# One product-key query over 512 tokens in place of two over 256, and gate steps twice as close

## The chip, the cores and the metric

The kernel runs on one core of one Trainium2 chip. The metric is device time in microseconds (us) of one execution. The kernel before takes 3155.48 us, the median of 3 runs (3149.81 to 3155.99).

The profile names the engines PE (matrix products; PEld its weight loads), DVE (VectorE), ACT (ScalarE), POOL (GpSimd) and SP (SyncE, which issues most transfers). Each works through its own instructions in order. L217 is line 217 of the kernel.

## The reference

One layer for a sequence of 1024 tokens with 1024 channels, in float32. The first half mixes tokens: a convolution group and a recurrent group (RWKV-7) read one input projection, and their outputs go through an output projection and a layer norm. The second half is a retrieval over 128 x 128 = 16384 one-neuron experts (PEER). Cut to what matters here:

```python
h2 = adaln(x, shift2, scale2)
q = (h2 @ peer_wq).reshape(bsz, seq, PEER_HEADS, PEER_QDIM).astype(jnp.float32)
...
s1 = jnp.einsum('bshd,hnd->bshn', q[..., :half], peer_k1.astype(jnp.float32))
s2 = jnp.einsum('bshd,hnd->bshn', q[..., half:], peer_k2.astype(jnp.float32))
v1, i1 = lax.top_k(s1, PEER_TOPK)
v2, i2 = lax.top_k(s2, PEER_TOPK)
cand = (v1[..., :, None] + v2[..., None, :]).reshape(bsz, seq, PEER_HEADS, PEER_TOPK * PEER_TOPK)
sc, ci = lax.top_k(cand, PEER_TOPK)
...
gates = jax.nn.softmax(sc, axis=-1)
...
    z = jnp.einsum('td,tkd->tk', hb, u_sel)
    act = jax.nn.gelu(z, approximate=False) * gb
    return jnp.einsum('tk,tkd->td', act, jnp.take(peer_v, eb, axis=0))
...
x = layer_norm(ALPHA * x + gate2[:, None, :] * y2, ln2_g, ln2_b)
```

The projection `h2 @ peer_wq` is 1024 x 2048. With 8 heads and two halves there are 16 score vectors of 128 for each token, the best 16 of each are kept, and from their sums the best 16 experts of a head.

## The kernel before

The tokens lie in 8 tiles of 128. Tiles 0 to 4 are *dense* (`DT`): all 16384 experts are computed for them, and a gate matrix that is zero but for the chosen experts picks. Tiles 5, 6 and 7 (`GT`) fetch the rows of their chosen experts one by one (`gather`). So the run has three parts: the front with the recurrence, a stage of fronts, queries, choices and gate matrices (some 900 to 1338 us), and the dense stage, in which PE computes over 128 blocks of experts and the gathers run beside it.

The work of the middle stage is written as Python generators, each of which yields after a few instructions.

- `front(t0, pg_)` (L829) takes 256 tokens (`PB`) from the mixers through the output projection (8 weight tiles of 1 MB, products of 512 columns at L867), two norms (L225, L247) and the scaling of the tiles that are fetched (L899). It leaves the normalised rows `xn` in `normed[t0]`. The last front, front(768), takes its pages from `page2`, the pool `pg2` of 12 pages. It yields some 197 times.
- `query(t0)` (L904) turns `xn` into channels (`to_channels`, L249: transposes at L255, the high and low part of each number at L258 and L259), and multiplies them with the 16 weight tiles of `wq`: `load_split` (L192) fetches a tile of 1 MB into one of three buffers (`WSPLIT`), `proj` (L210) makes 24 products of 256 columns from it at L217 (three for each of 8 channel blocks) and yields after each. After each group of four tiles come the scores (L939). For tiles up to 5 `best16` (L821: L823 to L827 on DVE) finds the best 16 of each score vector at once, with a yield after each; scores of tiles 6 and 7 go to memory (L944) and are looked at in the dense stage. At its end it hands `choose` of its tiles to the list `slow`. query(512) yields 417 times, query(768) 393 times.
- `choose(tt, ...)` (L965) finds the 16 best experts of each head on DVE and their gates. For tiles 4 and 5 its working pages come from `page2`. At the end of a dense tile's choice, `gate_matrix` of that tile is appended to the list `gates` (L1049). For tile 4, the last dense one, the gate matrix reads the choice from its pages; for the others it reads it back from memory.
- `gate_matrix(tt, chosen)` (L1053) has 32 steps for a tile of 128 tokens, 160 in all. A step makes masks (DVE, L1091), two operands from them (ACT at L1097 and L1100, POOL at L1098), four products (8 records of L1105, since they are in float32), and copies them out (ACT, L1106). Eight steps fill a stage of 2 MB, which ACT's queue writes to memory (L1113); the last block stays on chip (L1112).

After the recurrence the loop at L1179 drives all of this. Each turn makes one step of `side`, every second turn (`TSLOW`) one of `slow`, and every twelfth (`TGATE`) one of `gates`, the latter under a priority that is raised by 500 instructions (`GPRI`). Once `side` is empty each turn steps both lists. `side` holds what is left of the earlier work, then `beside(front(768), query(512))`, which steps the two in turn, and then query(768). The scheduler orders each engine's instructions by this order and by when their operands are expected; an instruction can thus be placed ahead of an earlier one that is not ready.

Behind the loop the pool `pg2` is closed, and `h2h` and `h2l`, the channels of the five dense tiles, are laid over the same space and loaded (L1194, 16 loads, not ahead of the fetch of tile 10 of `wq`). The dense stage splits the u weights into `uhi` and `ulo` (L1302 on ACT, L1304 on POOL), two buffers each, from three raw buffers. Its products are those of L1388 and L1404. The first block needs the gate values of all five tiles (L1392).

Of the kernel before, what the change touches and what calls it, by code (L numbers as in the profile page):

```python
# [11 lines left out]
F32R = mybir.dt.float32r  # L12
# [3 lines left out]
AF = mybir.ActivationFunctionType  # L16
# [5 lines left out]
S = 1024  # L22
D = 1024
KD = 8
# [16 lines left out]
PB = 256  # L41
# [31 lines left out]
RATES = 1.0, 0.5  # L73
NPAGE = 30
TSLOW = 2
TGATE = 12
CBUF = 4
GB = 2, 3
MB = 3
# [17 lines left out]
def layer_kernel(ctx, tc, x, cols, c_row, cond_w, w_in, w2a2, g2, w_out, ln_rows, wq, keys, peer_u, peer_ut, peer_v, peer_vt, out):  # L97
    nc = tc.nc
    V, A, G, T = nc.vector, nc.scalar, nc.gpsimd, nc.tensor
# [24 lines left out]
    mod = const.tile([128, 48], F32)  # L124
    modp = const.tile([128, 8, 2], F32)
# [58 lines left out]
    def page(name, dt=F32, w=512):  # L184
        return pgp.tile([128, max(w, 512)], dt, tag="pg", name=name)[:, :w]
# [63 lines left out]
    def to_channels(xn, shift, scale, hi, lo, keep=None, ks=range(KD), bank=None):  # L249

        n = 128 * len(xn)
        for k in ks:
            pt = (bank or mm)()[:, :n]
            for i, parts in enumerate(xn):
                T.transpose(pt[:, 128 * i:128 * i + 128], parts[k // 4][:, 128 * (k % 4):128 * (k % 4) + 128], ident)  # L255
            hf = page("hf", w=n)
            A.activation(hf, pt, AF.Identity, bias=shift(k), scale=scale(k))
            A.activation(hi[k], hf, AF.Copy)  # L258
            V.tensor_sub(lo[k], hf, hi[k].bitcast(F32))  # L259
            if keep:  # L260
                keep(k, hi[k], lo[k])
# [13 lines left out]
    def beside(a, b):  # L275

        a, b = [a], [b]
        while a or b:
            step(a)
            step(b)  # L280
            yield
# [330 lines left out]
    for l in range(6):  # L612
# [6 lines left out]
        nm = rc.tile([128, 64], F32, name=f"offm{l}", bufs=1)  # L619
# [9 lines left out]
    side, rate, credit, fills = [], [0.0], [0.0], [0]  # L629
# [21 lines left out]
    kept, ys, late, normed, page2, st3, blocks = {}, {}, [], {}, [], [], [0]  # L651
# [164 lines left out]
    def duo(name, dt=F32, pg_=page):  # L816

        ps = [pg_(name, dt).rearrange("p (a t) -> p a t", a=2) for _ in range(KD // 2)]
        return ps, [ps[k // 2][:, k % 2, :] for k in range(KD)]
# [81 lines left out]
                    ld(h2_d[tile0 + t][:, 512 * i:512 * i + 512], xt[i])  # L901
        normed[t0] = xn

    def query(t0):  # L904

        n, nt, tile0 = PB, PB // 128, t0 // 128
        fetch = [tile0 + t in GT for t in range(nt)]
        xn = normed.pop(t0)
        hi, lo = duo("h2hi", F32R)[1], duo("h2lo", F32R)[1]

        def keep(k, h, l):
            for w, f in enumerate((h, l)):
                for t in range(nt):
                    if not fetch[t]:
                        d = 128 * DT.index(tile0 + t)
                        ld(h2t_d[w, k, :, d:d + 128], f[:, 128 * t:128 * t + 128].bitcast(F32))

        to_channels(xn, lambda k: mod[:, 24 + k:25 + k], lambda k: modp[:, k, 1:2], hi, lo, keep)
        yield
        vi = [page("vi").rearrange("p (q h a r) -> p q h a r", q=2, h=NH, a=2) for t in range(nt)  # L920
              if tile0 + t not in score_d]
        val = [t[:, 0] for t in vi]
        idx = [t[:, 1].bitcast(U32) for t in vi]
        for g in range(4):
            kt = pgp.tile([128, 4, 128], F32, tag="pg", name="keys")
            ld(kt, keys[:, 4 * g:4 * g + 4, :])
            qt = []
            for m in range(4):
                w = load_split(wq, 4 * g + m)
                pt = mm(n)  # L930
                yield from proj(w, (hi, lo), pt)
                if m % 2 == 0:
                    qp = page("qt").rearrange("p (a t) -> p a t", a=2)
                A.activation(qp[:, m % 2, :], pt, AF.Copy)
                qt.append(qp[:, m % 2, :])
            for t in range(nt):
                ps = mm()
                for m in range(4):
                    T.matmul(ps[:, 128 * m:128 * m + 128], qt[m][:, 128 * t:128 * t + 128], kt[:, m, :],  # L939
                             start=True, stop=True)  # L940
                s = page("s12")
                A.activation(s, ps, AF.Copy)
                if tile0 + t in score_d:
                    ld(score_d[tile0 + t][g], s)  # L944
                    yield
                    continue
                for m in range(4):
                    best16(val[t][:, 2 * g + m // 2, m % 2], idx[t][:, 2 * g + m // 2, m % 2], s[:, 128 * m:128 * m + 128])
                    yield
        for t in range(len(vi)):  # L950
            slow.append(choose(tile0 + t, val[t], idx[t], 0, NH, 4, lambda nm, d, w, p=page2[0] if t0 == S - 2 * PB and P2C else page: p(nm, d, w), V if t0 >= LV else G))
# [170 lines left out]
    for c in range(16):  # L1122
# [17 lines left out]
        if flight:  # L1140
            f = flight.pop(0)
# [26 lines left out]
    de = ctx.enter_context(tc.tile_pool(name="de", bufs=1, side="right"))  # L1168
# [6 lines left out]
    pg2 = pg2x.enter_context(tc.tile_pool(name="pg2", bufs=NP2, side="right"))  # L1175
    page2.append(lambda name, dt=F32, w=512: pg2.tile([128, max(w, 512)], dt, tag="pg2", name=name)[:, :w])

    side += [beside(front(S - PB, page2[0]), query(S - 2 * PB)), query(S - PB)]
    while side or slow or gates:  # L1179
        step(side)  # L1180
        fills[0] += 1
# [186 lines left out]
    for g in range(32):  # L1368
# [6 lines left out]
        for e in range(4):  # L1375
# [7 lines left out]
            for bs in NBLK:  # L1383
                p = md(NW) if g == 0 and e < 3 and bs.start else mg(NW)
# [96 lines left out]
```

## Time and profile before

| what | value |
|---|---|
| median of 3 runs | 3155.48 us |
| the profiled execution's own time | 3159.3 us |
| its span, first to last instruction | 3157.5 us |
| busy in the span: PE, DVE, ACT, POOL | 94%, 76%, 37%, 57% |
| mean granted clock of PE | 0.959 |
| moved by DMA | 945.77 MB, mean 300 GB/s |

The profile shows one execution. A busy share is a mean over the whole span, and most of the span is the dense stage, so the middle stage has to be read from tables that are cut to it. In the views by line, L217 is both the input projection (512 columns) and the queries (256 columns); the shape tells them apart. Durations of PE's records overlap, since a product starts before the one ahead of it has ended: what a product costs is read from how many of them pass in a stretch, not from the duration of one.

### The profile page before, as it was taken

What the parts mean: (1) busy time and instruction counts of PE and PEld (TensorE: products, weight loads), DVE (VectorE), ACT (ScalarE), POOL (GpSimd) and SP (SyncE); (2) the same over time, 40 slices, a digit from 0 to 9 for tenths busy, and PEclk for the clock granted to TensorE, in tenths of its full rate; (3) what the DMA queues carried; (4) which work ended last, traced back from release to release, by engine and by line L of the source; (5) the groups of instructions that cost most, each with busy time, mean ns of one, the idle gap of its engine ahead of it and who ended that gap; (6) DMA issues with size and microseconds to landing.
All of it is one profiled execution on the core that took longest, in us unless ns stands there. A gap on an engine that the chain in (4) does not pass through costs nothing.

```text
span 3157.5 us, 54845 instructions
## 1 busy us (share of the span) xinstructions
PE 2966.5 (94%) x20416; PEld 2621.4 (83%) x20416; DVE 2388.5 (76%) x5388; ACT 1181.8 (37%) x2220; POOL 1815.5 (57%) x1419
## 2 busy tenths in 40 slices
PE   6979999989899889899999999999999999999996
PEld 4748667878778788898898888889899998999985
DVE  6276654447876989369989999887787877778789
ACT  5552442334345667742332323323222232222323
POOL 2433112224362443477777776877778678777874
PEclk9989999968888999999999999999999999999998
DMA  8878856768576998999999998999999989998995
GB/s 317 308 203 311 261 159 205 267 220 312 201 239 208 310 330 288 292 341 343 312 326 332 318 341 305 341 348 336 345 331 340 341 317 361 327 348 328 339 332 198
DMA packets 441579, 945.77 MB, mean 300 GB/s; under 512 B 92464, under 2 KB 242400, under 8 KB 419296
## 3 DMA queue, kind: packets, MB, share of 16 engines
q1 hardware_dynamic: 248480, 497.62, 45.8%
q0 software_dynamic: 110592, 402.70, 34.9%
q10 hardware_dynamic: 82240, 41.94, 4.8%
q8 instruction: 160, 2.62, 0.3%
q14 instruction: 107, 0.88, 0.1%
HBM read 800.76 MB, written 141.39 MB: 298 GB/s over the span
## 4 chain that ended last, share of the span: by engine, by line
PE 52%; DVE 19%; DMA 7%; issue 6%; POOL 4%; ACT 3%; SPq 0%; another core or an unknown queue 0%; ACTq 0%; POOLq 0%; DVEq 0%
PE mg L1388 18%; PE md L1404 17%; PE mm L217 5%; DVE grow L1267 3%; PE mm L867 2%; POOL grow L1259 2%; PE mm L525 2%; PE mgate L1105 2%; DVE gy L1274 2%; DMA cw<-cond_w 1%; DVE yacc L1422 1%; DMA grow<-peer_u,eid 1%; DVE mask L1091 1%; DMA vraw<-peer_vt 1%; DMA grow<-peer_v,eid 1%
## 5 line engine op out<-in xcount | busy, mean ns | idle before, releaser
L1388 PE MATMUL mg<-h2h,uhi 128*128 128x320 f32 x2024 | 626.9, 310 | 7.1 <-DVE al L1394 7.1
L1388 PE MATMUL mg<-h2h,ulo 128*128 128x320 f32 x2024 | 625.8, 309 | 1.8 <-POOL ulo L1304 1.6
L1388 PE MATMUL mg<-h2l,uhi 128*128 128x320 f32 x2024 | 626.0, 309 | 0.0
L1274 DVE SCALAR_TENSOR_TENSOR gy<-grow,gz,gy 128x1024 f32<-128x1024 f32 x381 | 487.7, 1280 | 18.0 <-DMA grow<-peer_v,eid 16.4
L1404 PE MATMUL md<-vhi,ah 128*128 128x512 f32 x1260 | 486.5, 392 | 5.8 <-ACT ah L1393 2.8
L1404 PE MATMUL md<-vlo,ah 128*128 128x512 f32 x1260 | 491.8, 391 | 0.0
L1404 PE MATMUL md<-vhi,al 128*128 128x512 f32 x1260 | 491.3, 391 | 0.0
L1267 DVE SCALAR_TENSOR_TENSOR grow<-grow,gh 128x1024 f32<-128x1024 f32 x384 | 460.8, 1211 | 36.9 <-DMA grow<-peer_u,eid 32.9
L1259 POOL DMA_INDIRECT grow<-peer_u,eid x384 | 362.5, 944 | 196.3 <-DVE grow L1267 73.7
L1259 POOL DMA_INDIRECT grow<-peer_v,eid x384 | 367.4, 957 | 185.3 <-DVE gy L1274 89.3
L1388 PEld LDWEIGHTS mg<-h2h,uhi 128*128 128x128 f32 x2024 | 380.4, 188 | 15.1 <-DVE al L1394 10.0
L1388 PEld LDWEIGHTS mg<-h2l,uhi 128*128 128x128 f32 x2024 | 380.4, 188 | 5.4
L1388 PEld LDWEIGHTS mg<-h2h,ulo 128*128 128x128 f32 x2024 | 380.3, 188 | 5.5 <-POOL ulo L1304 2.7
L1304 POOL TENSOR_TENSOR ulo<-uraw,uhi 128x1024 fp32r<-128x1024 f32 x128 | 310.0, 2422 | 34.8 <-ACT uhi L1302 29.1
L1304 POOL TENSOR_TENSOR vlo<-vraw,vhi 128x1024 fp32r<-128x1024 f32 x128 | 308.9, 2414 | 10.6 <-ACT vhi L1302 5.4
L1302 ACT ACTIVATE vhi<-vraw 128x1024 fp32r<-128x1024 f32 x128 | 135.2, 1056 | 425.1 <-DMA vraw<-peer_vt 382.7
L1422 DVE TENSOR_TENSOR yacc<-md,yacc 128x512 f32<-128x512 f32 x300 | 204.2, 685 | 115.9 <-PE md L1404 104.3
L1404 PEld LDWEIGHTS md<-vhi,ah 128*128 128x128 f32 x1260 | 236.5, 188 | 53.8 <-ACT ah L1393 4.3
L1404 PEld LDWEIGHTS md<-vlo,ah 128*128 128x128 f32 x1260 | 236.9, 188 | 49.1
L1098 POOL TENSOR_TENSOR ob<-mask,selt 128x384 f32<-128x384 bf16 x160 | 140.9, 894 | 237.9 <-DVE mask L1091 105.3
L1404 PEld LDWEIGHTS md<-vhi,al 128*128 128x128 f32 x1260 | 237.0, 188 | 45.2
L217 PE MATMUL mm<-hhi,wsplit 128*128 128x512 f32 x672 | 228.7, 414 | 8.4 <-ACT gsig L396 5.4
(415 smaller groups left out, 5660.6 us busy)
## 6 DMA issues: line engine op xcount, KB each, us to landing
uraw<-peer_ut SPq DMA_DIRECT2D x128, 512.0 KB
vraw<-peer_vt SPq DMA_DIRECT2D x128, 512.0 KB
wsplit<-split_wq SPq DMA_DIRECT2D x48, 1024.0 KB
G_d<-stage ACTq DMA_DIRECT2D x20, 2048.0 KB
gmat<-G_d SPq DMA_DIRECT2D x32, 1024.0 KB
cw<-cond_w SPq DMA_DIRECT2D x48, 512.0 KB
wsplit<-split_w_out SPq DMA_DIRECT2D x24, 1024.0 KB
split_w_in<-wsplit SPq DMA_DIRECT2D x22, 1024.0 KB
```

Of the source, the lines that this page charges most:

```text
L217: T.matmul(pt, l[:, k, :], r[k], start=i == 0, stop=i == 3 * KD - 1)
L525: T.matmul(pt[:, 128 * g:128 * g + 128], dg[:, 128 * j:128 * j + 128], ubuf[ct][:, g, LAGS - 1 - m:LAGS - 1 - m + 128], start=m == 0, stop ...
L867: T.matmul(acc[t], l[k][:, ts], r, start=k == 0 and q == 0, stop=k == KD - 1 and q == 2)
L1098: G.tensor_mul(ob[:, :3], mb[:, :3], gt[:, c:c + 3, None].to_broadcast([128, 3, 128]))
L1259: G.indirect_dma_start(out=r, out_offset=None, in_=peer_u if k < 128 else peer_v, in_offset=bass.IndirectOffsetOnAxis(ap=eid[:, k % 128:k ...
L1267: V.scalar_tensor_tensor(r, r, 1.0, ht, op0=OP.mult, op1=OP.mult, accum_out=z[:, i:i + 1])
L1274: V.scalar_tensor_tensor(y, r, z[:, i - 128:i - 127], y, op0=OP.mult, op1=OP.add)
L1302: A.activation(hi, raw, AF.Copy)
L1304: G.tensor_sub(lo, raw, hi.bitcast(F32))
L1388: T.matmul(p, l[:, k, :], r[k][:, bs], start=i == 0, stop=i == 3 * KD - 1)
L1404: T.matmul(p, l[:, ts], r[:, e % 2, :], start=e == 0 and q == 0, stop=e == 3 and q == 2)
L1422: ins = V.tensor_add(ya, p, ya)
```

## The change

The last two queries become one. `query` is split: `channels` makes the channels of 256 tokens, and `query` takes ready-made places for 512 (`made`). The channels of tokens 512 to 767 are made beside front(768); behind front(768) the query makes those of tokens 768 to 1023 and then runs over all 512 tokens, with products of 512 columns. Its high parts lie in the two `uhi` and two `ulo` buffers of the dense stage, its low parts in eight pages. Each of the 16 weight tiles is fetched once for both halves. The four score tiles of a group follow its four weight tiles, and `choose` of tiles 4 and 5 is handed to `slow` at the end of the merged query. `TGATE` goes from 12 to 6.

```diff
-TGATE = 12
+TGATE = 6
...
-    def query(t0):
-
-        n, nt, tile0 = PB, PB // 128, t0 // 128
+    def channels(t0, hi, lo):
+
+        nt, tile0 = PB // 128, t0 // 128
         fetch = [tile0 + t in GT for t in range(nt)]
-        xn = normed.pop(t0)
-        hi, lo = duo("h2hi", F32R)[1], duo("h2lo", F32R)[1]
...
-        to_channels(xn, lambda k: mod[:, 24 + k:25 + k], lambda k: modp[:, k, 1:2], hi, lo, keep)
-        yield
+        to_channels(normed.pop(t0), lambda k: mod[:, 24 + k:25 + k], lambda k: modp[:, k, 1:2], hi, lo, keep)
+        yield
+
+    def query(t0, made=None):
+
+        tile0 = t0 // 128
+        if made:
+            n, (hi, lo) = 2 * PB, made
+            yield from channels(t0 + PB, *([f[:, PB:] for f in fs] for fs in made))
+        else:
+            n, hi, lo = PB, duo("h2hi", F32R)[1], duo("h2lo", F32R)[1]
+            yield from channels(t0, hi, lo)
+        nt = n // 128
...
-                if m % 2 == 0:
-                    qp = page("qt").rearrange("p (a t) -> p a t", a=2)
-                A.activation(qp[:, m % 2, :], pt, AF.Copy)
-                qt.append(qp[:, m % 2, :])
+                if m * n % 512 == 0:
+                    qp = page("qt").rearrange("p (a t) -> p a t", t=n)
+                qt.append(qp[:, m % (512 // n), :])
+                A.activation(qt[m], pt, AF.Copy)
...
-    side += [beside(front(S - PB, page2[0]), query(S - 2 * PB)), query(S - PB)]
+    both = [], [page("qlo", F32R) for _ in range(KD)]
+    for nm in ("uhi", "ulo"):
+        for _ in range(2):
+            t_ = de.tile([128, KD, 128], F32R, name=nm, bufs=2).rearrange("p (a k) b -> p a (k b)", a=2)
+            both[0].extend(t_[:, i] for i in range(2))
+    side += [beside(front(S - PB, page2[0]), channels(S - 2 * PB, *([f[:, :PB] for f in fs] for fs in both))),
+             query(S - 2 * PB, both)]
```

## The prediction

> **What bounds the kernel now.** I read the busy table by stages first, cut where the work changes hands: 1020 (the recurrence ends), 1143, 1203 (the last query's products begin), 1299 (its last scores), 1338 (the dense stage runs steadily). The columns are the stretch, its length, then busy us of PE, weight load, DVE, ACT and POOL, the granted clock, the DMA share and GB/s.
>
> ```profile
> core 0: us, PE busy (x) PEld busy (x) DVE busy (x) ACT busy (x) POOL busy (x), PEclk, DMA share, GB/s
> 1020.00:1143.00 123.00, 103.70 (x698) 96.24 (x697) 110.90 (x415) 79.42 (x174) 56.29 (x55) 0.91 0.94 308
> 1143.00:1203.00 60.00, 54.03 (x438) 50.90 (x437) 56.64 (x280) 44.98 (x104) 23.93 (x26) 1.00 0.88 283
> 1203.00:1299.00 96.00, 87.04 (x734) 86.12 (x733) 64.19 (x209) 64.26 (x149) 35.98 (x41) 0.98 0.95 320
> 1299.00:1338.00 39.00, 34.93 (x257) 31.69 (x257) 14.40 (x22) 36.46 (x82) 21.71 (x25) 1.00 0.88 269
> 1338.00:3158.00 1820.00, 1777.74 (x9935) 1615.61 (x9934) 1521.02 (x2694) 517.92 (x852) 1357.62 (x1028) 0.99 0.91 328
> ```
>
> The reader is to see three things. The dense stage is PE's (1777.74 of 1820 us) and the change leaves it alone, so what counts is when it starts. From 1020 to 1203 VectorE is nearly full (110.90 of 123, then 56.64 of 60). From 1299 to 1338 ScalarE is (36.46 of 39). The chain of work that ended last says what starts the dense stage: the last gate step, and behind it the dense products in one run.
>
> ```profile
> 1336.70 1.13 PE mgate L1105 x8
> 1337.83 7.33 PE mg L1388 x50
> ```
>
> So I follow the gate steps (8 records of L1105 each). The same table for L1105 alone:
>
> ```profile
> 900.00:910.00 10.00, 3.48 (x24) 2.90 (x24) 1.00 0.73 234
> 910.00:1020.00 110.00, 31.09 (x213) 28.46 (x214) 0.91 0.72 233
> 1020.00:1130.00 110.00, 43.73 (x298) 41.16 (x297) 0.90 0.94 305
> 1203.00:1299.00 96.00, 40.18 (x308) 37.32 (x309) 0.98 0.95 320
> 1299.00:1338.00 39.00, 27.94 (x206) 24.56 (x205) 1.00 0.88 269
> 1313.40:1336.70 23.30, 20.31 (x145) 17.44 (x145) 1.00 0.83 248
> ```
>
> That is 30 of the 160 steps by 1020 (24 + 213 records), 67 by 1130, some 38 during the last query and 26 behind it. With nothing else to do (the last row) 18 steps take 23.3 us: 1.29 us a step, ScalarE's pace.
>
> **The change part by part.** *Products.* The paces come from the chain, whose columns are start, duration and what ran: 256 columns, 512 columns, a pair of gate steps, score products. The last two rows are of the stage table for L217 alone.
>
> ```profile
> 1222.88 2.87 PE mm L217 x24
> 1091.28 1.40 PE mm L867 x6
> 1225.75 1.79 PE mgate L1105 x16
> 1180.53 1.34 PE mm L939 x12
> 1203.00:1299.00 96.00, 51.53 (x359) 45.83 (x357) 0.98 0.95 320
> 1020.00:1143.00 123.00, 32.18 (x227) 30.09 (x228) 0.91 0.94 308
> ```
>
> A product of 256 columns takes 2.87/24 = 0.120 us, one of 512 takes 1.40/6 = 0.233, a gate step 0.895, a score record 0.112. Two queries are 2 x 16 x 24 = 768 products, 91.8 us; the merged one is 384 of double width, 89.6. PE gains 2 us: what is fetched once was not the cost on PE. The score products stay: 128 records, 14.3 us.
>
> *Fetches.* The two queries read 16 tiles each, the merged one 16 in all:
>
> ```profile
> wsplit<-split_wq SPq DMA_DIRECT2D x48, 1024.0 KB
> ```
>
> 16 x 1.05 MB = 16.8 MB go, 54 us of transfers at the 308 GB/s of the first stage. Today some nine of these tiles (227 products of 24 each) pass beside front(768), whose w_out tiles pass the same three buffers in turn, one of wq to one of w_out. So the front's products come sooner. I count only VectorE's wait for them, next.
>
> *The front is left alone.* Its normalised rows are what the second half of the merged query needs.
>
> ```profile
> L867 PE MATMUL mm<-wsplit,ychi x64: 387/396/774, 1027.5 to 1120.8; 128*128 128x512 f32 x64
> L871 DVE SCALAR_TENSOR_TENSOR xt<-xt,mm 128x512 f32<-128x512 f32 x4 | 2.7, 670 | 8.3 <-PE mm L867 8.3
> L247 ACT ACTIVATE xn<-xt,nbias,rstd x4: 802/808/816, 1142.2 to 1155.4; 128x512 f32<-128x512 f32 x4
> L823 DVE MAX8 vi<-s 128x8 f32<-128x128 f32 x16 | 3.6, 274 | 0.0
> L824 DVE FIND_INDEX8 vi<-vi,s 128x8 uint32<-128x128 f32 x16 | 4.4, 280 | 0.0
> L825 DVE MATCH_REPLACE8 s<-vi,s 128x128 f32<-128x128 f32 x17 | 4.6, 270 | 0.0
> L826 DVE MAX8 vi<-s 128x8 f32<-128x128 f32 x22 | 5.5, 273 | 0.0
> L827 DVE FIND_INDEX8 vi<-vi,s 128x8 uint32<-128x128 f32 x23 | 6.2, 279 | 0.0
> ```
>
> Now the rows are ready at 1156.2 (1155.4 and 0.8). The second row and the last five are from the groups of lines for 1020 to 1156: VectorE there ran 16 best16 of query(512), 3.6 + 4.4 + 4.6 + 16/22 of 5.5 + 16/23 of 6.2 = 21 us, with 3 us for value loads 24. They move behind the front. Its 8.3 us wait goes too. 1156 - 24 - 8 = 1124; 4 us for masks of gates that now come earlier (7 of the 29 more steps taken below, 0.63 each; the others I take as fitting in before 1020), 2 for the first transposed channel: the merged products start near **1130**. Today only 359 of the 768 are left at 1203, since 227 ran beside the front. That is the price: between 1020 and 1130 PE now has the front and gates alone. Bounds: 1105, if the front runs at PE's pace (96 x 0.233 = 22 us from 1027.5, then today's 35 us from 1121 to 1156, some waits), and 1156, if VectorE stays full.
>
> *Gates.* The loop made 417 + 393 = 810 iterations for the two queries (1 + 384 + 32, and 1 + 384 + 8), 67 gate steps at twelve; now 197 for the front and 425 for the query (1 + 384 + 40), 103 steps at six. But gate(2) and (3) wait for choose(2) and (3), and a step takes VectorE 0.63 us of mask (13.25/21, below). I take 96 of the 128 early steps done by 1130 (67 today; 128 at best), so 32 inside the query: 28.6 us of PE. The query then ends at 1130 + (89.6 + 14.3 + 28.6)/0.95 = **1269.5**; the 0.95 is between full and today's 88% (359 x 0.120 + 308 x 0.112 + 64 x 0.112 = 85 of 96 us).
>
> *What is late next.* Tile 4's last scores come with the last group, and gate(4) needs choose(4). Today they come at 1182, as the chain's score row shows, with query(768) still to run above the whole tail. The rows of its transposes, then of masks and of channels from 1182 to 1233:
>
> ```profile
> L1068 PE MATMUL selbank<-ident,tkg x3: 272/272/273, 1233.3 to 1233.8; 128*128 128x128 f32 x3
> 1182.00:1233.00 51.00, 13.25 (x21) 1.00 0.82 261
> 1182.00:1233.00 51.00, 3.94 (x8) 1.00 0.82 261
> ```
>
> 51 us less 13.25 and 3.94 is 34 us from last scores to gate(4), then 3 us for its first masks and copies (an estimate from 0.63 us a mask and 1.29 a step) and 32 steps of 1.29 = 41: **78 us** with PE almost idle, and an end at 1347.5. Today this tail lies beside query(768), and gates end 38 us after the last scores.
>
> *The dense operands.* choose(4) and choose(5) both take pages of pg2, under which h2h and h2l are laid; their 16 loads wait for choose(5), today at 1255, 22 us behind gate(4)'s transposes, and take 13 us:
>
> ```profile
> L1037 DVE TENSOR_TENSOR tkg<-oh x4: 210/212/213, 1253.9 to 1254.9; 128x64 f32<-128x64 bf16 x4
> L1194 SPq DMA_DIRECT2D h2h<-h2t_d x8: 320/374/739, 1278.1 to 1290.6; - x8
> 1299.00:1337.50 38.50, 7.79 (x48) 7.05 (x48) 1.00 0.89 272
> L1302 ACT ACTIVATE uhi<-uraw x4: 1050/1056/1060, 1043.3 to 1344.8; 128x1024 fp32r<-128x1024 f32 x4
> L1304 POOL TENSOR_TENSOR ulo<-uraw,uhi 128x1024 fp32r<-128x1024 f32 x128 | 310.0, 2422 | 34.8 <-ACT uhi L1302 29.1
> ```
>
> That is 34 + 22 + 13 = 69 us behind the scores, just inside the 78, so the 48 dense products that PE has now done ahead of 1337.5 (the third row, L1388 alone; 7.0 us at 7.33/50 each) are half lost: 3.5 us. If masks delay choose(5) by 13 us (21 of 0.63), the loads set the end. Behind the h2h loads on SP wait the loads of gate values and u tiles; ScalarE and POOL split u only when the query has left uhi and ulo (1.06 + 2.4 us of ACT and POOL, hidden under choose(4), 3.5 us if not), and the third raw load waits for that. ScalarE's q copies, four key loads fewer and h2 stores cost nothing: ScalarE has 32 us free in the last query's stage.
>
> *Sum.* Gates end at 1347.5, and with 3.5 that is 1351.0; today they end at 1336.70 + 0.9 = 1337.6: **+13.4 us**. The profiled execution took 3159.3 us (span 3157.5), 3.8 above the median of 3155.48; I move that median: **3169**.
>
> **A rule against it.** A wait shows in the clock already:
>
> ```profile
> 1288.09 0.58 PE L217 MATMUL mm<-h2hi,wsplit 128*128 128x256 f32 x1 [4.45 <-DMA wsplit<-split_wq]
> 1280.00:1300.00 20.00, 13.95 (x110) 13.58 (x109) 4.81 (x7) 10.02 (x24) 5.86 (x8) 0.91 1.04 377
> ```
>
> 4.45 us idle, and 0.09 x 20 / 0.5 = 3.6 us at half clock. The Trainium skill, "TensorE: Matmul & The Clock Gate", section "Part 1: The HAM clock gate", says that PE falls to half rate after an idle window of some 3.4 us and needs as long to come back; by that, and the trace agrees, the 34 us gap would start gate(4) at half clock. A step would be 1.79 us of PE for some four steps where ScalarE sets 1.29: 2 us more, 3171.
>
> **The rivals.** *Faster: gates end the kernel, and six frees them.* For it: today's last 26 steps run alone, and 54 us of transfers go. Against it: VectorE's 110.90 of 123. If the front runs at 1110 and 108 steps are done by then: 1110 + (103.9 + 17.9)/0.97 = 1235.5, tail 74: 1309.5, + 3.5, so -25: 3131. It wins from a query that ends before 1337.6 - 78 - 3.5 = 1256.
>
> *No change:* the query ends within 6 us of that 1256 (fourteen fewer steps inside it, or a start at 1117): 3149 to 3162. The fetches were hidden, and idle time only moved.
>
> *Much slower:* masks at the doubled pace go ahead of the norms, so the rows come at 1156 as today and the products start at 1160: the query ends at 1299.5, the loads behind choose(5) end 69 + 13 = 82 us later, 1381.5: +44, 3199.
>
> That the change doesn't halve the fetches can be ruled out: load_split is called 16 times in place of 32.
>
> **How the numbers follow.** Forecast (+6 to +30) 0.36, much slower 0.16, no change 0.17, faster 0.31. 0.2% is 6.3 us, about what a measurement can tell. Range: 3126 (the start at 1105, 16 steps inside, 0.97) to 3206 (the much slower case with the whole lead of 7.0 us lost); some 0.1 is left out on each side. The forecast's own range is 3162 to 3186. Slower 0.52, same 0.17, faster 0.31.
>
> **What would show it.** In the new profile L217's double products start near 1130 and end near 1270; no L1388 before gate(4) has begun; ScalarE full for some 41 us at the end; VectorE not full between 1130 and 1270; DMA share lower there. I am wrong if the products start before 1110, if gates 0 to 3 are done before the query starts, or if choose(4) takes well under 34 us.

## The result, and the profile after

| | before | after |
|---|---|---|
| median | 3154.47 us of 4 runs (3149.81 to 3155.99) | 3198.53 us of 4 runs (3192.5 to 3199.61) |
| the profiled execution, its span | 3159.3, 3157.5 us | 3198.3, 3196.6 us |
| mean granted clock of PE | 0.959 | 0.952 |

The change makes the kernel **slower by 44 us**: ratio 1.0146, 95% interval 1.0129 to 1.0162. (One run of before more than ahead of the prediction moves its median from 3155.48 to 3154.47.) The profiled executions lie 39 us apart, because before's was one of its longer runs. Lines in the new kernel are some 9 to 15 further down: gate products are L1114 (L1105 before), masks L1100, score products L948, the transposes at the head of a gate matrix L1077, the loads of h2h and h2l L1209, the dense products L1403 and L1419, the copy of gate products ScalarE makes into its stage L1115.

First the busy table by stages of the kernel after, with the columns of the prediction's first fence. It is cut where the work changes hands now: the merged query's products are about to begin (1130), its last scores (1279), the transposes of gate(4) (1312), the end of choose(5) (1340), the dense products in one run (1379).

```profile
core 0: us, PE busy (x) PEld busy (x) DVE busy (x) ACT busy (x) POOL busy (x), PEclk, DMA share, GB/s
1020.00:1130.00 110.00, 73.28 (x428) 63.04 (x426) 91.00 (x328) 77.22 (x167) 57.35 (x53) 0.83 0.81 259
1130.00:1279.00 149.00, 148.54 (x903) 131.72 (x904) 69.56 (x296) 89.12 (x192) 45.78 (x52) 0.99 0.65 206
1279.00:1312.00 33.00, 10.70 (x83) 9.49 (x81) 32.40 (x182) 15.19 (x33) 6.44 (x8) 0.80 0.48 138
1312.00:1340.00 28.00, 16.76 (x86) 14.93 (x87) 27.23 (x83) 17.02 (x39) 12.84 (x13) 0.68 0.32 114
1340.00:1379.00 39.00, 32.01 (x227) 30.04 (x226) 12.71 (x19) 28.90 (x65) 16.60 (x21) 0.91 0.94 298
1379.00:3197.00 1818.00, 1777.67 (x9935) 1616.81 (x9933) 1510.41 (x2694) 521.29 (x855) 1356.89 (x1028) 0.99 0.91 328
```

The reader is to see two halves. While the merged query runs, PE is full (148.54 of 149) and VectorE is half idle (69.56). When it ends, they change places: for 61 us VectorE is full (32.40 of 33, then 27.23 of 28) and PE does 27.46 us of work. The dense stage is the same 1777.7 us of PE as before; it only starts later. The chain of work that ended last has its start, to be set beside before's row at 1337.83:

```profile
1377.25 0.89 PE mgate L1114 x8
...
1378.72 7.33 PE mg L1403 x50
```

The dense run starts 40.9 us later, which is enough for the whole loss of the profiled execution (39 us). The same table for the gate products (L1114 alone, 8 records a step):

```profile
900.00:1130.00 230.00, 83.42 (x552) 76.74 (x552) 0.87 0.76 243
1130.00:1279.00 149.00, 48.62 (x384) 47.68 (x385) 0.99 0.65 206
...
1312.00:1340.00 28.00, 15.80 (x83) 14.59 (x84) 0.68 0.32 114
1340.00:1379.00 39.00, 25.49 (x175) 23.21 (x173) 0.91 0.94 298
```

At 1130 some 69 steps are done (552/8), two more than before at that time, though the loop offers one twice as often. And gate(4) makes only ten steps in its first 28 us.

Next the views by line, whose times are the starts of the first and the last instruction: the normalised rows, the products, the scores, the transposes of gate(4), its gate products, the last of choose(5), and the loads that wait for it.

```profile
L247 ACT ACTIVATE xn<-xt,nbias,rstd x4: 802/806/815, 1120.3 to 1123.8; 128x512 f32<-128x512 f32 x4
L217 PE MATMUL mm<-uhi,wsplit x128: 389/393/775, 1133.9 to 1268.9; 128*128 128x512 f32 x128
L948 PE MATMUL mm<-keys,qt x144: 271/275/377, 1004.0 to 1278.9; 128*128 128x128 f32 x144
L1077 PE MATMUL selbank<-ident,tkg x3: 421/473/477, 1311.9 to 1312.5; 128*128 128x128 f32 x3
L1114 PE MATMUL mgate<-oa,ob x288: 270/275/582, 1290.3 to 1377.9; 128*128 128x128 f32 x144
L1046 DVE TENSOR_TENSOR tkg<-oh x4: 209/210/210, 1337.5 to 1338.5; 128x64 f32<-128x64 bf16 x4
L1209 SPq DMA_DIRECT2D h2l<-h2t_d x8: 319/376/1176, 1344.2 to 1367.7; - x8
```

So the **tail** behind the last scores is 99 us long: choose(4) 33.0 us (1278.9 to 1311.9), gate(4) 66.0 us (to 1377.9). What VectorE does in the first 28 us of gate(4), from the groups of lines (the last column is its idle time before the group):

```profile
L1100 DVE TENSOR_TENSOR mask<-iota_b,selbank 128x1024 bf16<-128x1024 bf16 x13 | 8.6, 676 | 0.0
L1040 DVE TENSOR_TENSOR oh<-oh 128x512 bf16<-128x512 bf16 (+2 forms) x12 | 4.5, 409 | 0.0
L1034 DVE TENSOR_TENSOR oh<-oh,tkb 128x1024 bf16<-128x1024 bf16 x4 | 3.6, 946 | 0.0
L1029 DVE TENSOR_TENSOR oh<-iota_q,tkb 128x1024 bf16<-128x1024 bf16 x4 | 2.6, 685 | 0.0
```

Masks are 8.6 us of these 28. The rows L1040 to L1029, and smaller ones, are choose(5), which has come to lie on the same engine at the same time. Only 13 of gate(4)'s 32 masks are made there, and VectorE never waits (0.0): it is the bound. Behind it comes a second wait, in the chain of waits:

```profile
1349.24 18.44 DMA G_d<-stage
```

ScalarE waits 6.0 us there for a stage buffer (the view of waits), while the write of the gate matrix runs at the same time as the loads of h2h and h2l (DMA share 0.94 from 1340 to 1379).

### The profile page after: what moved, and what is told of

The parts are those of the page before. It is cut to its first block, busy times and chain, and to the rows that moved or that the text cites. A ratio compares the mean times of both kernels' runs of the same rounds, so it can differ in the third digit from the quotient of the medians.

```text
span 3196.6 us, 54042 instructions
## 1 busy us (share of the span) xinstructions
PE 2962.5 (93%) x20032; PEld 2605.0 (81%) x20032; DVE 2364.9 (74%) x5388; ACT 1187.0 (37%) x2207; POOL 1816.9 (57%) x1419
## 3 DMA queue, kind: packets, MB, share of 16 engines
q8 instruction: 157, 2.57, 0.3%
## 4 chain that ended last, share of the span: by engine, by line
PE 63%; DVE 15%; DMA 6%; issue 4%; ACT 2%; POOL 2%; SPq 0%; DVEq 0%; POOLq 0%; ACTq 0%
PE mg L1403 22%; PE md L1419 21%; PE mm L217 7%; PE mgate L1114 2%; PE mm L867 2%; DVE gy L1289 1%; PE mm L525 1%; DMA cw<-cond_w 1%; DMA grow<-peer_v,eid 1%; DVE mask L1100 1%; DVE grow L1282 1%; PE bank L704 1%; DMA grow<-peer_u,eid 1%; PE mm L948 1%; PE bank L730 1%
## 5 line engine op out<-in xcount | busy, mean ns | idle before, releaser
L1403 PE MATMUL mg<-h2h,uhi 128*128 128x320 f32 x2024 | 626.9, 310 | 3.1 <-DVE al L1409 3.1
L1403 PE MATMUL mg<-h2h,ulo 128*128 128x320 f32 x2024 | 626.2, 309 | 0.4 <-POOL ulo L1319 0.4
L1403 PE MATMUL mg<-h2l,uhi 128*128 128x320 f32 x2024 | 626.4, 310 | 0.0
L1289 DVE SCALAR_TENSOR_TENSOR gy<-grow,gz,gy 128x1024 f32<-128x1024 f32 x381 | 487.5, 1280 | 14.8 <-DMA grow<-peer_v,eid 13.2
L1419 PE MATMUL md<-vlo,ah 128*128 128x512 f32 x1260 | 491.4, 391 | 0.0
L1419 PE MATMUL md<-vhi,al 128*128 128x512 f32 x1260 | 491.3, 391 | 0.0
L1419 PE MATMUL md<-vhi,ah 128*128 128x512 f32 x1260 | 486.8, 392 | 4.4 <-ACT ah L1408 2.3
L1403 PEld LDWEIGHTS mg<-h2h,uhi 128*128 128x128 f32 x2024 | 381.0, 188 | 10.8 <-DVE al L1409 5.5
L1403 PEld LDWEIGHTS mg<-h2l,uhi 128*128 128x128 f32 x2024 | 380.9, 188 | 4.9
L1403 PEld LDWEIGHTS mg<-h2h,ulo 128*128 128x128 f32 x2024 | 380.8, 188 | 4.2 <-POOL ulo L1319 0.8
L1319 POOL TENSOR_TENSOR ulo<-uraw,uhi 128x1024 fp32r<-128x1024 f32 x128 | 309.0, 2415 | 38.1 <-ACT uhi L1317 30.9
L1317 ACT ACTIVATE vhi<-vraw 128x1024 fp32r<-128x1024 f32 x128 | 135.1, 1055 | 392.5 <-DMA vraw<-peer_vt 346.1
L1419 PEld LDWEIGHTS md<-vhi,ah 128*128 128x128 f32 x1260 | 236.4, 188 | 51.8 <-ACT ah L1408 3.2
L1419 PEld LDWEIGHTS md<-vlo,ah 128*128 128x128 f32 x1260 | 236.9, 188 | 49.0
L1419 PEld LDWEIGHTS md<-vhi,al 128*128 128x128 f32 x1260 | 237.0, 188 | 45.1
```

The costliest lines, as they stand in the source:

```text
L1289: V.scalar_tensor_tensor(y, r, z[:, i - 128:i - 127], y, op0=OP.mult, op1=OP.add)
L1317: A.activation(hi, raw, AF.Copy)
L1319: G.tensor_sub(lo, raw, hi.bitcast(F32))
L1403: T.matmul(p, l[:, k, :], r[k][:, bs], start=i == 0, stop=i == 3 * KD - 1)
L1419: T.matmul(p, l[:, ts], r[:, e % 2, :], start=e == 0 and q == 0, stop=e == 3 and q == 2)
```

## The experiments

Each ratio is against the kernel before on the same chip in the same series. The last four columns were read in each run as in the fence of starts above (us): the first product of 512 columns, the last score product, from there to the transposes of gate(4), and from these to its last gate product. Medians of before differ from series to series (3148.92 to 3155.64), so losses are compared, not times.

| run | median us | ratio, 95% interval | first product | last scores | choose(4) | gate(4) |
|---|---|---|---|---|---|---|
| after | 3198.53 | 1.0146 (1.0129 to 1.0162) | 1133.9 | 1278.9 | 33.0 | 66.0 |
| e1 | 3197.31 | 1.0148 (1.0125 to 1.017) | 1128.4 | 1272.8 | 34.6 | 66.1 |
| e2 | 3156.43 | 1.0024 (1.0006 to 1.0041) | – | – | – | – |
| e3 | 3240.27 | 1.028 (1.0261 to 1.03) | 1131.5 | 1276.2 | 25.5 | 52.9 |
| e4 | 3194.22 | 1.0133 (1.0112 to 1.0155) | 1128.9 | 1273.3 | 39.6 | 56.5 |
| e5 | 3193.49 | 1.0136 (1.0109 to 1.0163) | 1126.0 | 1270.4 | 39.7 | 55.7 |
| e6 | 3168.6 | 1.0047 (1.0026 to 1.0069) | 1059.6 | 1245.3 | 37.4 | 66.5 |
| e8 | 3151.27 | 0.9995 (0.9981 to 1.0008) | – | – | – | – |
| e9 | 3158.51 | 1.0017 (1.0002 to 1.0031) | – | – | – | – |
| e10 | 3200.49 | 1.0164 (1.0132 to 1.0196) | 1137.0 | 1281.4 | 35.7 | 45.5 |
| e13 | 3205.97 | 1.0187 (1.0157 to 1.0217) | 1136.3 | 1281.2 | 33.7 | 50.9 |
| e14 | 3169.85 | 1.0063 (1.0045 to 1.0082) | 1061.0 | 1245.1 | 38.1 | 48.2 |
| e15 | 3177.06 | 1.0064 (1.0044 to 1.0085) | 1130.4 | 1274.8 | 33.0 | 47.6 |
| e16 | 3151.14 | 0.9989 (0.997 to 1.0009) | 1054.7 | 1239.7 | 37.9 | 48.4 |

**The two parts of the change apart: e1 and e2.** The merged query with steps in twelve, and the two queries with steps in six.

```diff
-TGATE = 6
+TGATE = 12
```

> The merged query with gate steps every twelve turns. Theory (the chain behind the merged query's last scores sets the end: choose(4), then gate(4) beside choose(5)): the chain stays, and more steps of gates 0 to 3 are left when it begins, so no faster than the changed kernel and up to 25 us slower: 3198 to 3225 us. Rival (gate steps at six crowd VectorE ahead of the front and delay the query): 3165 to 3185 us, and the merged products start by 1120.

> The kernel before with gate steps every six turns, the merged query left out. Theory: gates 0 to 3 are through earlier, gate(4) starts soon after its choice at 1233 rather than at 1270, and the last scores near 1299 set the end: 3130 to 3150 us. Rival (steps at six crowd VectorE and PE): 3160 to 3180 us.

e1 loses as much as after: the chain that its theory named stays, but the further gate steps that it expected to be left over do not appear, and the time lies a little under its numbers. The gate products up to 1130 of e1:

```profile
900.00:1130.00 230.00, 82.30 (x557) 76.09 (x556) 0.90 0.75 243
```

and of e2:

```profile
900.00:1130.00 230.00, 82.90 (x578) 76.66 (x578) 0.92 0.81 267
```

In the merged kernel a step in twelve makes 557 records and one in six 552. In the kernel with two queries six makes 578 where twelve made 533 (24 + 213 + 298 by the prediction's rows, which count two on the cuts twice): under six steps more. The loop's count hardly sets the pace of the gates in these two kernels. e2 loses 0.24% where its theory expected a gain and its rival a larger loss. The loss is the merged query's.

**Moving work out of the tail: e3 and e4.** e3 sends tile 5's scores to memory, as those of tiles 6 and 7, so that its choice falls into the dense stage. e4 gives the choices of tiles 4 and 5 pages of the general pool, so that the loads of h2h and h2l need not wait for choose(5).

```diff
-for t in range(6, 8)}
+for t in range(5, 8)}
...
-P2C = 1
+P2C = 0
```

> The changed kernel, but tile 5's scores go to memory and its choice is made in the dense stage, as for tiles 6 and 7: 16 best16 and choose(5) leave VectorE's way behind the merged query. Theory: the last scores to gate(4) fall from 33 to some 27 us, gate(4) from 66 to some 45 to 50 us, and the loads of h2 come some 25 us earlier: 3170 to 3185 us. Rival (only the write of a stage that waits beside the h2 loads costs): 3190 to 3200 us.

> The changed kernel, but choose(4) and choose(5) take their pages from the large pool, so that the loads of h2 need not wait for choose(5). Theory (loads and gate writes meet in the tail, 18 us of the +44): the loads are issued before gate(4)'s stages are written, ACT's wait of 18 us for a stage goes: 3178 to 3188 us. Rival (choose(5) on VectorE is what slows gate(4), the loads cost nothing): 3194 to 3200 us.

In e3 the tail shrinks from 99.0 to 78.4 us, most of what its theory had (72 to 77), and the loss is 45 us larger than that of after (89.4 against 44.1): the choice is wanted at once by the first gather, so it runs in the dense stage, whose products need VectorE too. The busy table there:

```profile
1380.00:1440.00 60.00, 50.30 (x250) 43.92 (x248) 56.16 (x272) 24.75 (x43) 11.96 (x6) 0.91 0.24 79
```

PE has 50.30 of these 60 us where after has all 60.00, and its waits for VectorE and ScalarE from 1355 to the end are 36.8 us, 7.2 in after. In the profiled executions e3's dense run starts 24 us sooner (1354.6 against 1378.6), its last product starts 19 us later (3184.5 against 3165.5), and 62 us pass from there to the end of the span, where after has 31: the fetched tiles are late as well.

In e4 the loads pass at 1285 to 1295, gate(4) is 9.5 us shorter, and choose(4) 6.6 us longer: tail 96.1 in place of 99.0. The time is the rival's. VectorE remains full in gate(4)'s first 27 us:

```profile
1313.00:1340.00 27.00, 18.15 (x95) 16.10 (x96) 26.93 (x84) 18.60 (x41) 11.18 (x13) 0.69 0.16 44
1340.00:1370.00 30.00, 24.71 (x171) 21.81 (x170) 11.18 (x18) 27.32 (x62) 18.15 (x21) 0.94 0.86 266
```

And behind its last gate product (1369.4) the dense run does not follow at once, as the chain has it:

```profile
1361.18 8.67 DMA G_d<-stage
...
1369.86 2.57 DMA gmat<-G_d
...
1379.36 3.22 PE mg L1403 x22
```

A block of the gate matrix is written late (8.67 us), then read back (2.57), and the dense products that need it start 10 us behind gate(4). So next to nothing is left of the 9.5 us: the loss is 43.4 us where after's is 44.1.

**Holding choose(5) back: e5, e10, e13.** All with e4's pages. e5 writes choose(5)'s steps behind those of gate(4); e10 also orders VectorE's part of them behind the last mask; e13 is e10 with a third stage buffer for tile 4.

```diff
-        if fills[0] % TSLOW == 0 or not side:
+        if fills[0] % TSLOW == 0 if side else not gates or len(slow) > 1:
...
-                        V.tensor_tensor(m.rearrange("p t (e two) -> p t e two", two=2),
+                        mask_at[0] = V.tensor_tensor(m.rearrange("p t (e two) -> p t e two", two=2),
...
-            slow_step(1)
+            with nullcontext() if side or len(slow) > 1 else tc.issue_after(mask_at[0].ins): slow_step(1)
...
-            if st3 and tt != DT[-1] and blocks[0] % 3 == 0:
+            if st3 and blocks[0] % 3 == 0:
```

The first pair of lines is e5, the next two are added in e10, the last in e13.

> The kernel after, with the choices of tiles 4 and 5 on pages of the general pool (as in the run before, 3194.2 us) and, in the tail, choose(5) started only when the steps of gate(4) have been issued. Theory: gate(4) takes 57 us there because VectorE is full with choose(5) while it makes the masks (27 us for 92 records). Then the first 27 us shrink to some 15 and gate(4) takes 44 to 48 us; the dense products in one run start some 10 us earlier, 3180 to 3187 us. Rival: the writes of the gate matrix and ScalarE set the pace of gate(4); then it still takes 54 us or more and the time is 3190 to 3198.

> The kernel after, with the choices of tiles 4 and 5 on general pages, and all of VectorE's part of choose(5) ordered behind the last mask of gate(4). (In the run of 3193.5 us the steps of choose(5) were only written later in the program, and the scheduler put them among the masks all the same.) Theory: choose(5) on VectorE is what makes gate(4) slower than 1.29 us a step. Then gate(4) takes 42 to 47 us from its transposes to its last record (57 us in the run of 3194.2 us) and the dense run starts some 10 to 14 us earlier: 3180 to 3186 us, if the first gather can wait for choose(5), which ends some 25 us after gate(4). Rival: ScalarE and the writes of the gate matrix set the pace behind an empty VectorE; gate(4) then takes 52 us or more, 3190 to 3197 us.

> As the run ahead of this one, and the third stage buffer, which the tiles before take in turn, also for tile 4, so that its copies wait less for the writes of the gate matrix (the loads of the dense tiles' channels then wait for that buffer's write). Theory: the writes cost 5 to 15 us of the tail (chain rows of 12.89 and 8.67 us in the run of 3194.2 us): 3170 to 3180 us. Rival: the writes are late only because the steps are, and the loads come later: within 4 us of the run ahead, or slower.

e5 (3193.49) tells nothing: choose(5) still ended at 1336.1, beside gate(4), since the scheduler takes what is ready whatever the order in which it was written. e10 gives gate(4) the 45.5 us that its theory expected (42 to 47), and the time is 3200 all the same, 14 us above what it expected. More than the first gather, which its condition named, has to wait for choose(5). SyncE's timeline shows it (start, duration, instruction):

```profile
1374.08 0.33 SPq L1313 DMA_DIRECT2D vraw<-peer_vt  x1
1382.01 0.80 SPq L1021 DMA_DIRECT2D sel_d<-tkg  x2
1383.54 0.32 SPq L1259 DMA_DIRECT2D gsel<-sel_d  x1
1384.01 2.46 SPq L1342 DMA_DIRECT2D gmat<-G_d  x5
```

The gate values that the first dense block needs (L1342) are issued by SyncE behind the store of choose(5)'s result (L1021), which waits for choose(5) to end at 1382.0, and behind the first gather's load of it (L1259). The dense products stop until 1392, 29 us behind gate(4). e13 is slower still: the loads of h2h and h2l pass at 1350 to 1373 (1293 to 1303 in e10), behind the third buffer's write as was expected, and a write of the gate matrix takes 20.55 us in its chain: the rival's answer. Each of these moved a wait; none removed it.

**Leaving choose(5) out: e15.** e4 without choose(5): tile 5's experts are named by the best sub-keys of tile 4's scores, which stand ready as the query ends. So tile 5 fetches other experts than it should. (The lines are set out one below the other here; in the run the last of them stand on one line.)

```diff
+            if tile0 + t == 5:
+                p5 = page("s12").rearrange("p (w h r) -> p w h r", w=4, h=NH)
+                for w, f in enumerate((idx[0][:, :, 0], idx[0][:, :, 1], val[0][:, :, 0])):
+                    V.tensor_copy(p5[:, w], f)
+                for w in range(3):
+                    ld(sel_d[5][w], p5[:, w].rearrange("p h r -> p (h r)"))
+                continue
```

> The kernel after with the choices on general pages (3194.2 us), and choose(5) left out: tile 5 fetches experts named by the best sub-keys of tile 4's scores, which stand ready when the query ends. Theory: choose(5) beside gate(4) costs gate(4) some 8 us and nothing is queued behind it now: gate(4) takes 46 to 50 us as in the run that held it back, and no stall follows: the dense run starts 8 to 14 us earlier than at e4, 3178 to 3187 us. Rival: choose(5) hid under other waits (writes of the gate matrix): 3190 to 3197 us.

Its theory holds: gate(4) takes 47.6 us (46 to 50 expected), and the time is 1 us under what it gave. The dense run starts 24 us sooner than in e4 (1355.67 against 1379.36), more than the 8 to 14 expected, since choose(4) is shorter too and the late block is gone. The groups of lines for VectorE and ScalarE in gate(4) from 1308 to 1336, to be set beside those of after:

```profile
L1102 DVE TENSOR_TENSOR mask<-iota_b,selbank 128x1024 bf16<-128x1024 bf16 x20 | 13.0, 685 | 15.4 <-ACT ob L1111 9.5 <-POOL ob L1109 3.6 <-ACT selt L1082 1.5
...
L1108 ACT ACTIVATE oa<-mask 128x512 f32<-128x512 bf16 x18 | 11.4, 640 | 1.4 <-PE mgate L1116 1.3
```

Now VectorE waits for ScalarE (15.4 us of 28) and makes 20 masks where it made 13. gate(4) takes 47.6 us, the tail 80.6, and the dense run follows the last gate step without a gap:

```profile
1354.54 1.13 PE mgate L1116 x8
1355.67 7.33 PE mg L1405 x50
```

Against e4 the loss falls from 43.4 us (3194.22 less the 3150.85 of before in its series) to 21.4 (less 3155.64). So choose(5) in the tail of e4 costs 22 us, and the traces place it: 6.6 us ahead of gate(4) (39.6 to 33.0), 8.9 in it (56.5 to 47.6), and the late block's some 9 us behind it (the dense run 10 us after gate(4) in e4, under 1 here). In after it lies otherwise: choose(4) takes 33.0 us there as in e15, and the whole 18.4 us between the two tails (99.0 and 80.6) are gate(4)'s, with choose(5) and the loads in it together.

**The wait for the second half: e6, e14, e16.** Both halves of the merged query are the channels of tokens 512 to 767, so that it runs beside front(768). This leaves out the channels of tokens 768 to 1023. e14 adds e10's edit, e16 e15's.

```diff
-        to_channels(normed.pop(t0), lambda k: mod[:, 24 + k:25 + k], lambda k: modp[:, k, 1:2], hi, lo, keep)
+        xn = normed.pop(t0)
+        to_channels(xn, lambda k: mod[:, 24 + k:25 + k], lambda k: modp[:, k, 1:2], hi, lo, keep)
         yield
+        if twice:
+            to_channels(xn, lambda k: mod[:, 24 + k:25 + k], lambda k: modp[:, k, 1:2], *twice)
+            yield
...
-            yield from channels(t0 + PB, *([f[:, PB:] for f in fs] for fs in made))
...
-    side += [beside(front(S - PB, page2[0]), channels(S - 2 * PB, *([f[:, :PB] for f in fs] for fs in both))),
-             query(S - 2 * PB, both)]
+    side += [beside(front(S - PB, page2[0]), run([channels(S - 2 * PB, *([f[:, :PB] for f in fs] for fs in both),
+                                                              [[f[:, PB:] for f in fs] for fs in both]),
+                                                      query(S - 2 * PB, both)]))]
```

> The kernel after, but both halves of the merged query are the channels of tokens 512 to 767, so that the query need not wait for front(768) and runs beside it. It leaves out the channels of tokens 768 to 1023: tiles 6 and 7 get the scores of tiles 4 and 5. All else (16 weight tiles, 384 products of 512 columns, scores, choices, gates, gathers) is as in the kernel after. Theory: the price of the merge is the wait for the second half. Then the double products start between 1030 and 1060 us, the query ends by 1215, gate(4) no longer ends the stage alone, and the time is 3110 to 3150 us, under the kernel before. Rival: the merged query costs by itself, through its storage in the dense stage's buffers, its scores and both choices in one lump; then the tail behind the query stays near 100 us and the time is 3160 to 3200.

> The run with both halves of the query taken from tokens 512 to 767 (3168.6 us; it leaves out the channels of tokens 768 to 1023, tiles 6 and 7 get the scores of tiles 4 and 5), with choose(5) held behind the masks of gate(4) as in e10. Theory: query end and tail add up, whichever is shortened: the last scores at 1240 us and a tail of some 85 us put the dense run at 1325 to 1335, under the 1337.8 of before: 3143 to 3158 us. Rival: the tail there is not set by choose(5), 3162 to 3175 us.

> The run with both halves of the query from tokens 512 to 767 (3168.6 us; it leaves out the channels of tokens 768 to 1023, tiles 6 and 7 get the scores of tiles 4 and 5), and choose(5) left out as in e15. Theory: the last scores at 1240 us and a tail of 34 + 50 us put the dense run at 1326 to 1334, some 18 us before that run's 1350: 3145 to 3156 us, level with the kernel before or under it. Rival: something else ends last, 3160 us or more.

In e6 the products start at 1059.6, 74 us sooner than in after, but the last scores come only 33.6 us sooner (1245, where the theory had 1215), since PE is nearly full then too (183.63 of the 191 us from 1055 to 1246), with the front and the gates beside the query. Of the 44 us 29.3 go (loss 14.7); the rest stays, for the tail is 103.9 us long. The numbers are the rival's, yet two thirds of the loss is the theory's wait: each had half of it. e14 repeats e10: gate(4) takes 48.2 us, then the dense products wait for choose(5) until 1361, and the loss is 20.9; its theory fell with e10's. e16 takes both prices out. Its busy table over gate(4), then the end of its chain:

```profile
1278.00:1327.00 49.00, 41.19 (x287) 36.60 (x287) 21.83 (x32) 45.26 (x102) 28.09 (x33) 0.96 0.73 225
```

```profile
1325.17 1.13 PE mgate L1119 x8
1326.30 7.33 PE mg L1409 x50
```

ScalarE has 45.26 of 49 us, VectorE 21.83. The time is level with before (0.9989, the interval holds 1), so the two prices make up the whole loss: 29.3 + 22 = 51, where 44 + 4.5 = 48.5 went. (They do not add exactly: from e6 to e16 it is 19.2 us, 14.7 and 4.5.) The dense run of that profiled execution starts 11.5 us ahead of before's; the medians don't show so much.

**A stall of before: e8 and e9.** The kernel before, with its h2h and h2l loads held behind the last weight tile; e9 also with e4's pages.

```diff
-HP = 'wq', 10
+HP = 'wq', 15
```

> The kernel before, with the 16 loads of the dense tiles' channels held behind the fetch of the last weight tile of the query in place of that of tile 10. In before they pass at 1278 to 1291 us, ahead of weight tiles, and a product waits 4.45 us for its tile at 1288 at a granted clock of 0.91. Theory: this stall goes and comes back nowhere, since the loads are needed only near 1315 us: 3142 to 3150 us. Rival: the loads are then late for the dense products that PE does ahead, and the last gate step sets the end as before: 3152 to 3160.

> The kernel before, with the loads held behind the last weight tile as in the run ahead of this one, and the choices of tiles 4 and 5 on pages of the general pool, so that the loads wait for nothing but that fetch. Theory: 0 to 3 us less than the run ahead of this one, 3140 to 3150 us. Rival: the pages of the general pool are wanted by the query's scores and values, which then wait: 3155 to 3170.

From 1280 to 1300 PE is now busy 19.24 us where it was 13.95, so the 4.45 us wait for a weight tile is gone. But the theory's "comes back nowhere" fails: up to 1280.7 PE waits 5.04 us for a copy of ScalarE, and from 1260 to 1280 it is busy 15.64 us where before has 20.00. The time falls between what the two expected: twelve runs give no difference that can be told (0.9995, interval 0.9981 to 1.0008). In e9 PE has neither wait in the last query and its gates (the longest is 2.0 us), and it is if anything slower, as its rival's numbers had it. No run of this study beats the kernel before with the whole computation in it.

## Why the prediction was wrong in size

The direction and the place were right, the size was not: +13.4 us forecast, +44 measured. Step by step:

- *The front sooner, products at 1130.* Right within 4 us. The working had the rows at 1124, or 1128 with the masks, and the products at 1130; they came at 1124.6 (1123.8 and 0.8) and 1133.9.
- *96 of 128 early steps done by 1130.* Wrong: 69. The step took the loop's doubled count for a pace. e1 shows the same number at twelve, so the count did not set it; what did, masks or operands, was not tried. That put 48 steps into the query in place of 32 (384/8), 14.3 us of PE at 0.895 each. The products also began 3.9 us late, but PE was fuller than the 0.95 assumed (148.54 of 149), which gave some of that back: the last scores came at 1278.9 in place of 1269.5, 9.4 us late. Some ten of gates 0 to 3's steps were still left then (80 records from 1279 to 1312).
- *34 us from last scores to gate(4).* Right in the number, 33.0, with some luck: the 34 held no mask, and seven masks of earlier gates (4.7 us of VectorE) lay in the 33.0.
- *3 + 32 x 1.29 us for gate(4), the step that failed.* 66.0 us in place of 44, the largest miss of the sum: the pace was taken as ScalarE's, with VectorE as good as free. The 1.29 was read from a stretch in which VectorE had 14.40 of 39 us to do; the same prediction put choose(5) on VectorE 22 us into gate(4), asked only what it would do to the loads, and did not charge it to the masks. The other part is that the loads are late and meet the write of the gate matrix: put at 13 us, they took 24 (1343.8 to 1367.7). With the loads moved away gate(4) takes 56.5 us (e4), and with choose(5) left out as well 47.6 (e15), near the 44 forecast.
- *3.5 us of the lead lost.* Didn't happen. From 1340 to 1378.7 PE did 49 dense products between the gate steps, as many as before did ahead of 1337.5:

```profile
1340.00:1378.70 38.70, 11.31 (x49) 8.11 (x50) 0.91 0.95 300
```

- *The sum.* 9.4 + (99.0 - 78) - 3.5 = 27 us more than forecast, 40 in all, against 40.9 of the dense run.
- *The rivals.* "Much slower" named the time, 3199, with another mechanism: rows at 1156 and a late query, where the rows came at 1124.6. "Faster" and "no change" fell with the tail: the query end that they needed, 1256, is 1337.6 - 99 = 1239 by the measured tail. e6 ended its query at 1245.3, well under 1256, and still lost 14.7 us; e16, with a tail of 86.3, broke even from 1239.7.
- *The signs.* Those on VectorE, the DMA share and the first dense products came true. ScalarE, to be full for some 41 us at the end, had 45.92 of 67 (17.02 of 28, then 28.90 of 39): in the first part it was not the bound.
- *Half the clock behind the gap.* The trace shows the fall: behind 16.4 us without a product the transposes of gate(4) took 421 to 477 ns, where before's row has 272, and the granted clock is 0.68 from 1312 to 1340. The 2 us that the prediction made of it are not to be seen: in that stretch VectorE is full (27.23 of 28 us) and PE is busy for 16.76, so PE did not set the pace. What the fall costs where VectorE is free is separated by no run. The rows of the transposes of e14 and then of e16 differ, but both have dense products ahead of gate(4), both have a low clock in its first 12 us (0.72 and 0.83), and gate(4) takes 48.2 and 48.4 us:

```profile
L1080 PE MATMUL selbank<-ident,tkg x3: 273/329/332, 1283.2 to 1283.8; 128*128 128x128 f32 x3
```

```profile
L1082 PE MATMUL selbank<-ident,tkg x3: 421/474/476, 1277.6 to 1278.3; 128*128 128x128 f32 x3
```

The Trainium skill, "TensorE: Matmul & The Clock Gate", section "Part 1: The HAM clock gate", has PE at half rate after an idle window of some 3.4 us. In after the trace agrees: PE's last product of gates 0 to 3 ends at 1295.5, and the granted clock falls at 1299.0. In e16 it does not, and the measurement decides: the clock is 1.00 from 1274.5 to 1275.0 and 0.50 from 1275.5, with PE idle for under 1 us; in the 3.4 us up to 1275.15 PE was busy 1.98. So PE need not have been idle for the whole of such a window.

What stays open is how the 66.0 us split between choose(5) and the loads when both are there. Without the loads gate(4) is 9.5 us shorter, without both 18.4, but e4 made choose(4) longer by 6.6 at the same time, and no run leaves out choose(5) alone. The runs with both halves from one set of channels, and those without choose(5), leave work out: their times show what a wait costs and are not kernels to be had. That the choice of tile 4 alone could be started sooner, from scores that come group by group, was not tried.

## What to carry to other kernels

Before two pieces of work are merged so that an operand is fetched once, ask what the first piece's result was feeding while the second ran: here the chain behind tile 4's scores, 99 us in the merged kernel, lay under the other query, and merging laid it bare. A pace read from a stretch holds only for the engines that were free in it; when a tail is moved, list everything that comes due in it on each engine, and charge each to all the others. And a wait taken from one place is worth nothing until the next wait, and what is queued behind it (SyncE in e10, VectorE in e3), has been looked for.

## What was not expected of the hardware and the program

- Halving the weight fetches changed the DMA share during the query (0.65, where before had 0.95 in its last query) and brought nothing that shows: PE was the full engine there (148.54 of 149 us; 87.04 of 96 in before's last query), and its products cost the same (a product of 512 columns takes as long as two of 256, within 3%).
- The order in which steps are written says little about when they run: e1 and after, with steps offered at half or double the rate, differ by 5 records of 557, and in e5 an instruction written behind gate(4) still ran inside it.
- Taking a wait of 4.45 us from PE did not help: e8 got one of 5.04 us in its place, and in e9, which has neither, the dense run starts 8.8 us sooner than in before (1329.08 against 1337.83) and twelve runs show no gain. The times of e8 alone lie between 3144.9 and 3160.3.
